# A transformer trunk on one core: a scheduler's table of durations is corrected, and the steps of the attention block stand in another order

## The chip, the core and the metric

The kernel runs on one core of one Trainium2 chip. The metric is the device time of one execution in microseconds (us). The core's engines are TensorE (PE in the profile; its weight loads are PEld), VectorE (DVE), ScalarE (ACT), GpSimd (POOL) and SyncE (SP, which issues the transfers). Each of them works through its own instructions in the order in which the kernel lists them, and waits where an instruction needs what another engine has not yet made.

## The reference, cut to what matters

Two layers over 256 tokens of width 1024. Both begin and end with a half-step SwiGLU (width 2816). Between these, layer 0 has a gated linear recurrence, layer 1 a differential attention whose keys and values come from the stream behind layer 0. The change moves the steps of this attention:

```python
q = (h @ w_q).reshape(B, S, N_HEADS, 2, HEAD_DIM)
q = apply_rope(rmsnorm(q, q_norm), cos, sin) * (HEAD_DIM ** -0.5)
...
        scores = jnp.einsum('bhcqd,bhckd->bhcqk', qb, k, preferred_element_type=jnp.float32)
        p = jax.nn.softmax(jnp.where(mask, scores, -jnp.inf), axis=-1)
        attn = p[:, :, 0] - lam * p[:, :, 1]
        return jnp.einsum('bhqk,bhkd->bhqd', attn, vf)
...
    o = rmsnorm(o, sub_norm, SUBLN_EPS) * (1.0 - lambda_init)
    return o.reshape(B, S, D_MODEL).astype(h.dtype) @ w_o
```

There are 8 heads of 2 maps each (c = 0 and 1 above), so every head has two softmaxes.

## The kernel before

Every weight is read once, in pieces of 128x2048 floats (`raw`), by transfers that SyncE issues. Each half piece (a granule) is split into a high and a low part: ScalarE casts it (`whi`), VectorE subtracts (`wlo`). TensorE multiplies the high part with both parts of the activations and the low part with the high one. Six granules fit at a time.

The program is written twice. In a first pass a `Recorder` takes down every instruction of four engines and SyncE with what it depends on, and a planner (`plan`) runs through them: it keeps a clock for each engine, computes from `cost` how long an instruction holds its engine (`pitch`) and when its result is there (`lat`, with 94 ns to reach another engine), and among what could start within 60 ns takes the instruction with the longest work behind it. Instructions of one engine count as following each other at their pitch, except where the pair is in `op.raw`: then the second waits for the first one's result. In the second pass the instructions are issued in the order so found. So the durations in `cost` set the order on every engine, and nothing else: they compute nothing.

What `cost` cannot set is which tiles come to life in which order, and so which share a buffer. This is the program's order, and in the attention block it is `ATT_STEPS`, a list written by hand:

- `Q0`, `Q1`, `K0`, `K1`, `V0`, `V1`: a projection for heads 0 to 3 or 4 to 7, both halves of the tokens, 48 matmuls of 512 columns into two banks. Behind a Q or K projection ScalarE and VectorE norm and rotate the result (`qk_post`), and TensorE transposes it, four transposes for each half of the tokens. GpSimd's power gives the factor of the norm (`fac`, `facq`).
- `S0` to `S5`: scores and softmax. S0 and S3 are the first 128 tokens for heads 0 to 3 and 4 to 7; S1, S2, S4 and S5 the last 128 tokens for two heads each (0 and 1, 2 and 3, 4 and 5, 6 and 7). Scores go into two banks, one for each map. VectorE writes the mask and takes the maxima (`mx`), ScalarE has one exponential for each head and map, with the factor and the maximum as operands of one number per token and with a sum taken along; VectorE joins the two maps, TensorE transposes the result, and ScalarE copies it out.
- `A0` to `A6`: probabilities times values for two heads (`av`), 6 matmuls; then four squares with a sum on ScalarE, a power on GpSimd (`ofr`), four scaled copies on ScalarE, four transposes on TensorE.
- `O0` to `O7`: what 128 rows of the output projection give, 8 times 3 matmuls of 256 columns. O0 and O1 need A0, O2 and O3 need A2, and so on. The last two come behind the list.

The buffers in which TensorE's results stand are eight banks: six named `mm`, two named `aux`. All instructions carry one line of the kernel, that of the helper which issues them (L379; the changed kernel is one line shorter there, so L378), so that the tiles tell them apart.

Of the kernel before, what the change touches and what calls it, by code (L numbers as in the profile page):

```python
# [32 lines left out]
    "G3m M0 E3 D1 H4a M1 M2 E4 M3 H6m O0 M4 E5 M5 W W O1 E6 M6 E7 O2 O3 M7"  # L33
).split()
ATT_STEPS = (
    "Q0mm K1mm K0mm S1mm Q1mm S0mm V0mm A0 S2mm A2 S3mm V1mm S4mm S5mm O0 A4 O1 A6 O2 O3 O4 O5"
).split()
REC_OUT = "0m 1m 23m 45m 67s"
ATT_OUT = "0m 1m 23m 45m 67s"
# [55 lines left out]
def is_ap(v):  # L95
    return hasattr(v, "tensor") and hasattr(v, "ap")


def width(v):
    n = 1  # L100
    for _, c in v.ap[1:]:
        n *= c
    return n
# [12 lines left out]
def sources(a, k):  # L116
    vals = list(a if "out" in k else a[1:]) + [v for n, v in k.items() if n not in ("out", "accum_out")]
    return [v for v in vals if is_ap(v)]


def cost(op):
    k, out = op.k, op.outs[0] if op.outs else None
    ins = sources(op.a, k)
    psum = [v for v in ins if v.space == bass.MemoryType.PSUM]
    n = width(out) if out is not None else 1
    if op.eng == "tensor":
        if op.fn == "transpose":
            return 109, 220
        m = width(k["rhs"])
        if k["rhs"].dtype == BF16:  # L130
            return m / 2.4 + 3, m / 2.4 + 175
        if k["rhs"].dtype == F32R:
            return 0.4508 * m + 2.6, 0.4508 * m + 165
        p = 4 * m / 2.4 + 3 if m > 8 else 222
        if k["lhsT"].ap[0][1] <= HD:
            p /= 2
        return p, p + 170
    if op.eng == "scalar":
        if op.fn == "preload_act_table":
            return 1294, 1283  # L140
        scaled = is_ap(k.get("scale")) or is_ap(k.get("bias"))
        p = n / 1.2 + ((65 + 20 * scaled) if psum else (100 + 85 * scaled))
        lat = n / 1.2 + (172 if psum else 195 + 90 * scaled)
        return (p + 93, lat + 200) if len(op.outs) > 1 else (p, lat)
    if op.eng == "vector":
        if op.fn in ("reduce_sum", "reduce_max"):
            n = width(ins[0])
        if op.fn == "tensor_copy":
            return n / 1.92 + 67, n / 1.92 + 155
        if op.fn == "memset":  # L150
            return n / 0.96 + 10, n / 0.96 + 50
        if op.fn == "tensor_tensor_scan":
            return n * 2 / 0.96 + 55, n * 2 / 0.96 + 140
        rate = 0.96
        if op.fn == "tensor_scalar" and not psum:
            rate = 1.92
        scalar = op.fn in ("tensor_scalar", "scalar_tensor_tensor") and len(ins) > (1 if op.fn == "tensor_scalar" else 2)
        return n / rate + (125 if scalar else 68), n / rate + (210 if scalar else 153)
    if op.eng == "gpsimd":
        if op.fn == "memset":  # L160
            return 30, 100
        if k.get("op") == ALU.pow:
            return 300 + 170 * n, 340 + 170 * n
        return 120 + 2.14 * n, 160 + 2.14 * n
    return 420, 0


class Recorder:
# [16 lines left out]
    def add(self, eng, fn, a, k):  # L185
        op = Op()
# [11 lines left out]
        for v, w in [(v, False) for v in ins] + [(v, True) for v in op.outs]:  # L198
# [9 lines left out]
            for j, l, h, ww in self.hist[name]:  # L208
                if (w or ww) and l < hi and lo < h:
                    self.depend(op, j)  # L210
                    if ww and not w:
                        op.raw.add(j)
            if w:
                self.hist[name] = [x for x in self.hist[name] if not (lo <= x[1] and x[2] <= hi)]
            self.hist[name].append((op.i, lo, hi, w))
# [944 lines left out]
```

## Time and profile before

| | |
|---|---|
| three timed runs | 941.09, 941.13, 947.8 us; median 941.13 |
| the execution in the profile | 941.77 us, of which its span (first to last instruction) is 939.9 |
| TensorE busy | 930.3 us, 99% of the span |
| VectorE, ScalarE, GpSimd busy | 77%, 62%, 3% |
| granted TensorE clock, mean | 0.998 |
| attention block on TensorE | from 636.71 us (first projection) to 751.77 us (first matmul of the last SwiGLU) |

Two matmuls that follow each other overlap, and their ends are modelled, so the busy share of TensorE says little of how fast it works; but where a row says that it was idle and for whom it waited, nothing ran on it. The distance from one matmul's start to the next one's is what a matmul costs.

### The profile page before, as it was taken

Reading aid. Unit: us, or ns where it says so; the run is one execution under the profiler, and the core shown is the slowest. Engines: PE = TensorE matmul, PEld = TensorE weight load, DVE = VectorE, ACT = ScalarE, POOL = GpSimd, SP = SyncE. Lnnn points to the kernel's source line nnn. Section 1 sums busy time; section 2 is a strip of 40 time slices with the busy share of each in tenths; the row PEclk is TensorE's granted clock in tenths of the full one; section 3 lists DMA queues with packets and bytes.
Section 4 is the critical chain, followed back from the end, with each engine's and each line's share of the span. In section 5 each row is a group of like instructions: output and inputs, shape, how many; then the busy total and the mean of one; then the engine's idle time right before and its main releaser. Section 6 shows DMA issues by size and latency. Waiting matters only on the chain.

```text
span 939.9 us, 14667 instructions
## 1 busy us (share of the span) xinstructions
PE 930.3 (99%) x5586; PEld 824.5 (88%) x5586; DVE 723.9 (77%) x1226; ACT 581.2 (62%) x1039; POOL 31.9 (3%) x42
## 2 busy tenths in 40 slices
PE   8999999999999999999999999999999999999998
PEld 7888888899998888888888888888877988888887
DVE  7898887679898888866688887667996598888651
ACT  7666565569975656555566556555579766565541
POOL 0200000000000000000000000001310000000000
PEclk9999999999999999999999999999999999999999
DMA  8755556534375555555555555555533445555540
GB/s 318 246 201 196 180 183 237 208 136 141 132 266 180 182 193 205 182 179 192 203 186 182 182 191 201 189 179 179 179 135 97 164 175 194 180 184 201 204 158 17
DMA packets 25991, 172.33 MB, mean 183 GB/s; under 512 B 3136, under 2 KB 4288, under 8 KB 5568
## 3 DMA queue, kind: packets, MB, share of 16 engines
q1 hardware_dynamic: 25920, 171.39, 52.0%
q8 instruction: 44, 0.72, 0.3%
q14 instruction: 27, 0.22, 0.1%
HBM read 170.33 MB, written 1.05 MB: 182 GB/s over the span
## 4 chain that ended last, share of the span: by engine, by line
PE 95%; ACT 3%; DVE 1%; DMA 0%; issue 0%; SPq 0%; ACTq 0%
PE mm L379 92%; PE aux L379 3%; ACT w L379 2%; ACT b L379 1%; DMA xa<-xT 0%; ACT whi L379 0%; DVE wlo L379 0%; ACT L379 0%; DVE mx L379 0%; DVE w L379 0%; ACT xs L379 0%; DVE xs L379 0%; DVE xa L379 0%; SPq L379 0%; DVE mm L379 0%
## 5 line engine op out<-in xcount | busy, mean ns | idle before, releaser
L379 PE MATMUL mm<-xs,whi 128*128 128x512 f32 (+1 forms) x1632 | 531.6, 378 | 2.0 <-DVE xs L379 2.0
L379 DVE TENSOR_TENSOR wlo<-raw,whi 128x1024 fp32r<-128x1024 f32 (+1 forms) x321 | 391.0, 1220 | 132.8 <-ACT whi L379 132.2
L379 ACT CAST whi<-raw 128x1024 fp32r<-128x1024 f32 (+1 forms) x321 | 335.5, 1047 | 200.5 <-PE mm L379 180.5
L379 PE MATMUL mm<-xs,wlo 128*128 128x256 f32 x1520 | 426.2, 281 | 0.0
L379 PEld LDWEIGHTS mm<-xs,whi 128*128 128x128 f32 x1632 | 298.9, 188 | 60.3 <-DVE xs L379 2.3
L379 PE MATMUL mm<-b,whi 128*128 128x512 f32 (+1 forms) x982 | 292.7, 359 | 0.3 <-ACT w L379 0.2
L379 PEld LDWEIGHTS mm<-xs,wlo 128*128 128x128 f32 x1520 | 287.9, 190 | 0.5
L379 PE MATMUL mm<-b,wlo 128*128 128x256 f32 x832 | 233.2, 281 | 0.0
L379 PEld LDWEIGHTS mm<-b,whi 128*128 128x128 f32 x982 | 174.7, 189 | 29.1 <-ACT w L379 0.9
L379 PEld LDWEIGHTS mm<-b,wlo 128*128 128x128 f32 x832 | 157.6, 189 | 0.0
L379 ACT ACTIVATE w<-mm 128x256 f32<-128x256 f32 x207 | 79.5, 385 | 115.4 <-PE mm L379 110.8
L379 DVE TENSOR_TENSOR w<-mm,w 128x256 f32<-128x256 f32 x176 | 73.5, 421 | 27.1 <-ACT w L379 27.0
L379 DVE TENSOR_TENSOR w<-w,rb 128x512 f32<-128x512 f32 x88 | 60.2, 687 | 0.4
L379 DVE TENSOR_TENSOR w<-w,w 128x256 f32<-128x256 f32 (+2 forms) x104 | 45.2, 440 | 0.6 <-ACT w L379 0.6
L379 PE MATMUL mm<-whi,xk 128*128 128x512 f32 x128 | 42.1, 400 | 0.0
L379 ACT ACTIVATE w<-w 128x256 f32<-128x256 f32 x88 | 36.5, 418 | 3.3 <-DVE w L379 2.9
L379 DVE TENSOR_TENSOR b<-w,b 128x256 fp32r<-128x256 f32 x88 | 36.4, 417 | 1.9 <-ACT b L379 1.9
L379 ACT CAST b<-w 128x256 fp32r<-128x256 f32 x88 | 35.4, 406 | 2.9 <-DVE w L379 2.8
L379 DVE SCALAR_TENSOR_TENSOR xa<-mm,xa 128x256 f32<-128x256 f32 x32 | 13.5, 423 | 26.8 <-PE mm L379 18.4
L379 PEld LDWEIGHTS mm<-whi,xk 128*128 128x128 f32 x128 | 24.0, 188 | 4.7
L379 PE MATMUL mm<-wlo,xk 128*128 128x512 f32 x64 | 25.2, 394 | 0.0
L379 ACT ACTIVATE xs<-xa,vt 128x256 fp32r<-128x256 f32 x40 | 19.7, 504 | 8.9 <-DVE xa L379 8.7
(124 smaller groups left out, 483.8 us busy)
## 6 DMA issues: line engine op xcount, KB each, us to landing
raw<-wts SPq DMA_DIRECT2D x159, 1024.0 KB, 4.8
raw<-wts SPq DMA_DIRECT2D x3, 512.0 KB, 7.3
outT<-xa SPq DMA_DIRECT2D x8, 128.0 KB, 2.0
xa<-xT SPq DMA_DIRECT2D x3, 256.0 KB, 6.5
raw<-wts SPq DMA_DIRECT2D x2, 256.0 KB, 4.4
rw<-rows SPq DMA_DIRECT2D x1, 320.0 KB, 4.9
xa<-xT SPq DMA_DIRECT2D x1, 260.0 KB, 4.3
ident<-eye SPq DMA_DIRECT2D x1, 64.0 KB, 8.6
```

The lines of the kernel that those rows point to most:

```text
L379: getattr(getattr(self.nc, op.eng), op.fn)(*op.a, **op.k)
```

## The change

In `cost` the numbers of four kinds of instruction are replaced: matmuls on split weights, ScalarE operations with operands of one number per token (each such operand now counts 83 ns in the pitch, where before the first or only one counted 20 ns on a source in a bank and 85 ns on one in SBUF, and a second one nothing), VectorE's memset, and with it the results' times. In `Recorder.add` every pair of accesses to the same tile of which one writes is now in `op.raw`, where before a pair was there only if the first wrote and the second read. And `ATT_STEPS` has the same 22 steps in another order.

```diff
 ATT_STEPS = (
-    "Q0mm K1mm K0mm S1mm Q1mm S0mm V0mm A0 S2mm A2 S3mm V1mm S4mm S5mm O0 A4 O1 A6 O2 O3 O4 O5"
+    "K0mm K1mm Q0mm Q1mm S1mm S0mm V0mm S4mm A0 S2mm S3mm A2 V1mm A4 S5mm O0 O1 O2 A6 O3 O4 O5"
 ).split()
...
         if k["rhs"].dtype == F32R:
-            return 0.4508 * m + 2.6, 0.4508 * m + 165
+            return 0.4428 * m + 3.3, 0.4428 * m + 165
...
-        scaled = is_ap(k.get("scale")) or is_ap(k.get("bias"))
-        p = n / 1.2 + ((65 + 20 * scaled) if psum else (100 + 85 * scaled))
-        lat = n / 1.2 + (172 if psum else 195 + 90 * scaled)
+        scalars = is_ap(k.get("scale")) + is_ap(k.get("bias"))
+        p = n / 1.2 + (65 if psum else 100) + 83 * scalars
+        lat = n / 1.2 + (172 if psum else 195) + 93 * scalars
         return (p + 93, lat + 200) if len(op.outs) > 1 else (p, lat)
...
         if op.fn == "memset":
-            return n / 0.96 + 10, n / 0.96 + 50
+            return max(15, n / 0.96 - 60), n / 0.96 + 40
...
                 if (w or ww) and l < hi and lo < h:
                     self.depend(op, j)
-                    if ww and not w:
-                        op.raw.add(j)
+                    op.raw.add(j)
```

What this does to the order is seen best at three places of the attention block. The numbers in the names only tell tiles apart, and differ between the two kernels.

The first place is ScalarE behind the projection V0. In the kernel before, `mm_1525` and `mm_1526` are the scores of S2, `mm_1541` and `mm_1542` those of S3, and `aux_1519` is the result of A0, whose scaled copies (`ofr`) are what TensorE transposes next:

```order
L379 ACTIVATE w_3_1529,sm_1528<-mm_1525,mx_1527,facq_0_1387 128x256
L379 ACTIVATE w_4_1522,oss_1520<-aux_1519,ra_1504 128x128
L379 ACTIVATE w_4_1522,oss_1520<-aux_1519,ra_1472 128x128
L379 ACTIVATE w_4_1522,oss_1520<-aux_1519,ra_1504 128x128
L379 ACTIVATE w_4_1522,oss_1520<-aux_1519,ra_1472 128x128
L379 ACTIVATE w_3_1529,sm_1528<-mm_1525,mx_1527,facq_0_1387 128x256
L379 ACTIVATE w_0_1530,sm_1528<-mm_1526,mx_1527,facq_0_1387 128x256 x2
L379 ACTIVATE w_5_1545,sm_1544<-mm_1541,mx_1543,facq_0_1388 128x128 x4
L379 ACTIVATE w_2_1546,sm_1544<-mm_1542,mx_1543,facq_0_1388 128x128 x4
L379 ACTIVATE w_4_1522<-aux_1519,ofr_1523 128x128 x4
```

In the changed kernel `mm_1519` and `mm_1520` are the scores of S4, `mm_1535` and `mm_1536` those of S2, `mm_1544` and `mm_1545` those of S3, and `aux_1529` is the result of A0:

```order
L378 ACTIVATE w_5_1523,sm_1522<-mm_1519,mx_1521,facq_0_1388 128x256 x2
L378 ACTIVATE w_1_1532,oss_1530<-aux_1529,ra_1504 128x128
L378 ACTIVATE w_1_1532,oss_1530<-aux_1529,ra_1494 128x128
L378 ACTIVATE w_1_1532,oss_1530<-aux_1529,ra_1504 128x128
L378 ACTIVATE w_1_1532,oss_1530<-aux_1529,ra_1494 128x128
L378 ACTIVATE w_2_1524,sm_1522<-mm_1520,mx_1521,facq_0_1388 128x256 x2
L378 ACTIVATE w_3_1539,sm_1538<-mm_1535,mx_1537,facq_0_1387 128x256 x2
L378 ACTIVATE w_0_1540,sm_1538<-mm_1536,mx_1537,facq_0_1387 128x256 x2
L378 ACTIVATE w_1_1532<-aux_1529,ofr_1533 128x128 x3
L378 COPY b_0_1528<-aux_1527 128x512
L378 ACTIVATE w_1_1532<-aux_1529,ofr_1533 128x128
L378 ACTIVATE w_4_1548,sm_1547<-mm_1544,mx_1546,facq_0_1388 128x128 x4
```

The four copies of A0 stood behind the eight exponentials of S3 and stand ahead of them now; S4's four exponentials, which came after V1 before, have been put in ahead of S2's.

The second place is TensorE in V0 (`mm_1507`, `mm_1508`), where the transposes of S0's probabilities (`aux_1506`) come in. Before:

```order
L379 MATMUL mm_1508<-wlo_1511,xk_644 128x512
L379 MATMUL mm_1508<-whi_1510,xk_644 128x512
L379 MATMUL aux_1506<-ident_79,w_2_1502 128x128
L379 MATMUL mm_1507<-wlo_1513,xk_644 128x512
L379 MATMUL aux_1506<-ident_79,w_2_1502 128x128
L379 MATMUL mm_1507<-whi_1512,xk_644 128x512
L379 MATMUL aux_1506<-ident_79,w_2_1502 128x128 x2
```

Now:

```order
L378 MATMUL mm_1508<-wlo_1511,xk_644 128x512
L378 MATMUL aux_1506<-ident_79,w_4_1502 128x128
L378 MATMUL mm_1508<-whi_1510,xk_644 128x512
L378 MATMUL aux_1506<-ident_79,w_4_1502 128x128 x2
L378 MATMUL mm_1507<-whi_1512,xk_644 128x512
L378 MATMUL aux_1506<-ident_79,w_4_1502 128x128
L378 MATMUL mm_1507<-wlo_1513,xk_644 128x512
```

They come behind V0's 41st matmul, and came behind its 37th. The transposes of S1's probabilities and of Q1's second half, which before came behind the 20th and the 27th, come behind the 32nd and 33rd now.

The third place is TensorE right behind the scores of S0 (`mm_1498`, `mm_1499`). Before, V0 follows at once, and the first transposes of Q1's result come 19 matmuls later:

```order
L379 MATMUL mm_1499<-b_0_1383,b_0_1381 128x128
L379 MATMUL mm_1498<-b_0_1383,b_0_1381 128x128
L379 MATMUL mm_1499<-b_0_1383,b_0_1381 128x128
L379 MATMUL mm_1507<-whi_1484,xk_644 128x512
L379 MATMUL mm_1507<-wlo_1485,xk_644 128x512
```

Now the first transposes of Q1's result (`aux_1482`) stand between:

```order
L378 MATMUL mm_1499<-b_0_1383,b_0_1381 128x128
L378 MATMUL mm_1498<-b_0_1383,b_0_1381 128x128
L378 MATMUL mm_1499<-b_0_1383,b_0_1381 128x128
L378 MATMUL aux_1482<-ident_79,w_1_1480 128x128 x4
L378 MATMUL mm_1507<-whi_1474,xk_644 128x512
```

So a step of VectorE that has Q1's result to rotate is waited for 19 matmuls earlier. Outside the attention block TensorE's order differs in some 30 rows of the recurrent block and in a few of the SwiGLU blocks; ScalarE's and VectorE's differ by neighbours that change places, and SyncE's transfers come in the same order throughout.

## Rows read from the trace of the kernel before

**Rows 1.** The page: TensorE's busy time; shares of the chain that ended last.

```profile
PE 930.3 (99%) x5586; PEld 824.5 (88%) x5586; DVE 723.9 (77%) x1226; ACT 581.2 (62%) x1039; POOL 31.9 (3%) x42
...
PE 95%; ACT 3%; DVE 1%; DMA 0%; issue 0%; SPq 0%; ACTq 0%
```

**Rows 2.** Busy time by stretch: length, each engine (instructions), granted clock, DMA.

```profile
0.00:12.00 12.00, 8.98 (x39) 6.99 (x40) 6.33 (x15) 8.40 (x16) 0.34 (x6) 0.86 0.82 284
12.00:660.00 648.00, 647.92 (x3905) 578.31 (x3904) 513.78 (x844) 406.21 (x687) 16.12 (x25) 1.00 0.55 193
660.00:700.00 40.00, 39.06 (x200) 31.25 (x199) 37.75 (x79) 26.67 (x52) 10.74 (x6) 1.00 0.42 148
700.00:720.00 20.00, 18.25 (x111) 14.69 (x111) 14.34 (x40) 16.98 (x55) 2.01 (x2) 1.00 0.45 156
720.00:740.00 20.00, 19.71 (x161) 18.27 (x158) 12.20 (x32) 17.72 (x52) 1.01 (x1) 1.00 0.32 109
740.00:939.90 199.90, 196.40 (x1182) 175.02 (x1180) 139.49 (x219) 105.20 (x184) 1.70 (x2) 1.00 0.47 164
```

**Rows 3.** Timeline of TensorE around V0's end: start, length, operation [idle before <- releaser].

```profile
697.47 0.30 PE L379 MATMUL aux<-ident,w 128*128 128x128 f32 x1 [0.78 <-DVE w L379]
...
700.26 0.40 PE L379 MATMUL mm<-whi,xk 128*128 128x512 f32 x1
700.59 2.02 PE L379 MATMUL mm<-b,b 64*128 64x256 f32 x24
702.54 1.60 PE L379 MATMUL aux<-b,b 128*128 128x128 f32 x12
703.90 0.48 PE L379 MATMUL mm<-whi,xk 128*128 128x512 f32 x1
...
711.15 0.85 PE L379 MATMUL aux<-ident,w 128*128 128x128 f32 x3 [1.75 <-ACT w L379]
```

**Rows 4.** Timeline of ScalarE in V1: S2's first exponential to A0's copies.

```profile
703.58 0.56 ACT L379 ACTIVATE w<-mm,mx,facq 128x256 f32<-128x256 f32 x1 [1.26 <-DVE mx L379]
...
704.18 0.37 ACT L379 ACTIVATE w<-aux,ra 128x128 f32<-128x128 f32 x1
...
706.65 0.58 ACT L379 ACTIVATE w<-mm,mx,facq 128x256 f32<-128x256 f32 x1
...
707.20 0.48 ACT L379 ACTIVATE w<-mm,mx,facq 128x128 f32<-128x128 f32 x1
...
710.67 1.20 ACT L379 ACTIVATE w<-aux,ofr 128x128 f32<-128x128 f32 x4
711.67 1.14 ACT L379 CAST whi<-raw 128x1024 fp32r<-128x1024 f32 x1
...
713.18 0.70 ACT L379 COPY b<-aux 128x512 f32<-128x512 f32 x1
```

**Rows 5.** Timeline of TensorE: SwiGLU (56 pairs of matmuls between the first two), a projection.

```profile
25.25 0.39 PE L379 MATMUL mm<-xs,whi 128*128 128x512 f32 x1
...
44.66 0.39 PE L379 MATMUL mm<-xs,whi 128*128 128x512 f32 x1
...
637.18 0.62 PE L379 MATMUL mm<-whi,xs 128*128 128x512 f32 x2
...
646.73 0.62 PE L379 MATMUL mm<-whi,xs 128*128 128x512 f32 x2
```

**Rows 6.** Timeline of TensorE in V0: transposes between matmuls.

```profile
690.72 0.60 PE L379 MATMUL aux<-ident,w 128*128 128x128 f32 x4
691.07 0.48 PE L379 MATMUL mm<-whi,xk 128*128 128x512 f32 x1
691.39 0.83 PE L379 MATMUL aux<-ident,w 128*128 128x128 f32 x4
```

**Rows 7.** Timeline of VectorE: two products on Q1's first half, the second one in place.

```profile
684.33 0.69 DVE L379 TENSOR_TENSOR w<-w,gs 128x512 f32<-128x512 f32 x1
685.05 0.69 DVE L379 TENSOR_TENSOR w<-w,gc 128x512 f32<-128x512 f32 x1
```

## The prediction

> **What bounds the kernel now.** I read the page first: TensorE is busy 99% of the span, and 95% of the chain that ended last is its own work [rows 1]. So a gain can only come from time in which TensorE stands still, or from fewer changes between kinds of matmul on it. The busy times by stretch say where it stands still [rows 2]. From 12 to 660 us it is idle for 0.08 us in 648. At the start it is idle for 3.02 us and at the end for 3.50 (the first transfers and the last stores, whose instructions the change leaves in their order). In between lie three stretches of the attention block: 0.94 us in 660 to 700, 1.75 in 700 to 720 and 0.29 in 720 to 740, together **2.98 us**. That is all that the change can win back in idle time, 0.3% of the kernel.
>
> The timeline of TensorE names the two large pieces [rows 3]. At 697.47 S0's transposes waited 0.78 us for VectorE, which joins the two maps once ScalarE's exponentials are done. At 711.15 A0's transposes waited 1.75 us for ScalarE. The timeline of ScalarE says why [rows 4]: A0's four copies began at 710.67, directly behind S3's eight exponentials, which had held ScalarE since 707.20, and nobody waited for those eight.
>
> **Whether the new durations are the traced ones.** S3's eight exponentials took 710.67 - 707.20 = 3.47 us, 0.434 each [rows 4]. The old formula gives 128/1.2 + 65 + 20 + 93 = 285 ns, the new one 128/1.2 + 65 + 2 x 83 + 93 = 431. An exponential of 256 columns took 0.55 [rows 4], by the formulas 391 and 537 ns. Four scaled copies took 1.00 us; old 4 x 192 = 0.77, new 4 x 255 = 1.02. So the old planner believed that S3's exponentials took 8 x 0.149 = 1.2 us less than they do, and put A0's copies behind them. That is the hole at 711.15. A pair of SwiGLU matmuls took 19.41 us / 56 = 346.6 ns [rows 5]; old 351.4, new 346.7. An overwrite in place on the same engine began 0.72 us after the instruction that still read the data, which is 0.69 long [rows 7]: it waits for the result, as the new rule has it. The numbers are better ones, and they meet the mistake that made the large hole.
>
> **What goes.** Where V1 runs, ScalarE now has S4's and S2's exponentials, then A0's copies, then S3's. I check that A0's copies come in time by summing from V0's end. In the trace V0's last matmul starts at 700.26 and takes 0.23, so its end is 700.49, and the first exponential of the next softmax starts at 703.58, 3.1 us later [rows 3, 4]; S4 has the same chain of mask and maximum before it. Then come 8 exponentials of 0.55 and 4 squares of 0.37 [rows 4], 5.9 us, so that the copies begin 9.0 us behind V0's end; four of them take 1.0, and the copy of S4's probabilities between them about 0.5, so the last is done at 10.5. TensorE reaches A0's transposes after the scores of S4, S2 and S3 (8 matmuls of 256 columns and 8 of 128; 4 and 8 of these take 2.02 us [rows 3], so about 3.0), A0's six (703.90 - 702.54 = 1.36), 26 of V1's matmuls at 9.55 us / 42 = 0.227 [rows 5], which is 5.9, and S4's four transposes (691.07 - 690.72 = 0.35 [rows 6]): 10.6 us. That is 0.1 us behind the last copy: this hole closes, with nothing to spare. S0's transposes stand behind four more matmuls of V0 (0.9 us against a wait of 0.78), and what stood ahead of them on ScalarE and VectorE is the same: this hole closes as well. The rest of the 2.98 us are pieces of 0.1 to 0.2; I let them go too. **Term A: -2.98 us.**
>
> **What comes.** (1) TensorE changes from matmuls to transposes more often: in the attention block 29 times by the order, 25 before. Such a change costs the matmul ahead 691.39 - 691.07 - 0.227 = 0.09 us [rows 6]. **Term B: 4 x 0.09 = +0.36.** (2) Q1's first transposes now stand directly behind the scores of S0. The last matmul of Q1's first half ends 3 x 0.227 = 0.68 us ahead of Q1's end. Behind it follow ScalarE's copy (0.70 [rows 4]), two products (0.72 each) and a sum (0.69) on VectorE [rows 7]; the order puts two short masks ahead of the sum, and with these and the ways between engines I add 0.6, an estimate. 0.70 + 1.44 + 0.69 + 0.6 - 0.68 = 2.75 us behind Q1's end, against 2.02 us of scores: TensorE waits 0.7. The least is nothing (the masks start late, so the sum may pass early); the most is about 1.7, if VectorE is still held by the factor that it gets from GpSimd. **Term C: +0.7.** (3) Elsewhere each group of transposes has cover by the same kind of sum, but little of it (0.1 to 0.4 us at A0's and S4's groups in V1, at A2's, A4's and S5's in the output projection). **Term D: +0.2**, between 0 and 1.5.
>
> **What costs nothing.** In the SwiGLU blocks the order changes between neighbours on ScalarE and VectorE; TensorE was idle for 0.08 us in 648 there [rows 2], because a granule is split while earlier ones are still used, and a neighbour's 0.4 us does not reach that cover. In the recurrent block two groups of small matmuls stand some 24 matmuls later; what ScalarE makes of them came 6 us later anyhow, and the block had no hole to win. K0 ahead of Q0 changes which of two ready inputs is read first, and GpSimd's powers follow: K's four come first, then that of the stream's norm, then Q's; between Q0's end and the first use of its factor, in S1's maxima, lie Q1's 48 matmuls (10.9 us). SyncE's transfers keep their order, and none is waited for in the block.
>
> **Sum.** -2.98 + 0.36 + 0.7 + 0.2 = -1.7 us. Against the profiled execution's own 941.77 us (span 939.9 and 1.87 around it) that is 940.1; that execution lies 0.64 above the median of the runs, 941.13, so I forecast **939.4**.
>
> **The rivals.** *The holes only move* (0.22): the cover in V1 and in the output projection was 0.1 to 0.4 us in my sums; if five of these places miss by 0.3 each and C is 1.2, then C and D are 2.7 us in place of 0.9, and the time is 941.2. For it speaks that ScalarE is busy 85% of the stretch in which the holes lie [rows 2]; against it that the planner now counts the same durations as the trace.
>
> *Slower, since ScalarE comes late through V1* (0.1): S4's four exponentials (2.2 us) are new ahead of S3's. By the sum above S3's exponentials end 10.5 + 3.5 = 14.0 us behind V0's end, and the joined map is there some 0.8 later, at 14.8; TensorE comes to its transposes after 44 of V1's matmuls, 3.0 + 1.36 + 10.0 + about 1.3 for twelve transposes = 15.7. The cover is 0.9 us. Since the transposes stand between A2's matmuls, TensorE can do nothing else there. From 0.9 + 1.7 = 2.6 us of lateness on the kernel is slower than before; at 4 us, as from three casts of 0.95 that get ahead or from a late factor for heads 4 to 7 (S4 is the first to need it, 10 us earlier than before), it is 939.4 + 3.1 = 942.5.
>
> *A lost clock* (0.03): from 0 to 12 us the mean granted clock is 0.86 [rows 2], which is a part of the stretch at the lower of the two levels, 1.2 GHz, behind an idle piece of TensorE; in the attention block it stays at 1.00 through the hole of 1.75 us. If the new order has an idle piece that brings the clock down once, then 0.14 x 2 x 12 = 3.4 us run at half speed, which costs 1.7 us: 941.1. The Trainium skill's page "TensorE: Matmul & The Clock Gate", Part 1 (The HAM clock gate), has it that the clock is halved after an idle spell and comes back with sustained work; by that rule a hole of 1.75 us could have cost as much again, and closing it would give back 1.7 us more, but the trace shows no such loss there.
>
> *It does not do what it says* (0.05): the same waits appear under other names, and the time stays at 941.1. Against it stands that A0's copies have changed sides with S3's exponentials.
>
> **How the numbers follow.** The forecast has 0.6, its own range is 938.1 (A alone, with a little more from the recurrent block) to 940.5. For 8 in 10 I take in the case of moved holes and most of the slower one: 937.6 to 942.5. One per cent is 9.4 us, about what a measurement of this kernel can tell from no change. All the idle time inside the kernel is less than a third of that, so faster by over 1% has 0.01. For slower by over 1% TensorE would have to stand still for four times what it does now in that block; I leave 0.03. Within 1%: 0.96.
>
> **What would show it.** In the changed kernel's profile: idle time of TensorE from 660 to 740 us of about 1 us instead of 2.98; no wait for ScalarE of over 0.5 us at A0's transposes; a wait of 0.3 to 1 us at the transposes behind S0's scores; the first matmul of the last SwiGLU near 750 us instead of 751.77; the other stretches as they are. I am wrong if a wait of over 1 us stands in V1 or in the output projection, if the granted clock falls below 1.00 between 20 and 930 us, or if TensorE is idle in the SwiGLU blocks.

## The result, and the profile after

The changed kernel takes 936.76 us in the median of its executions (935.07 to 939.56), the kernel before 941.50 in the same comparison (940.74 to 947.8). The ratio is 0.9947, with a 95% interval of 0.9932 to 0.9962. That is 4.7 us less where 1.7 were forecast, and 0.84 us below the lower end of the wider range (937.6). The traced execution of the changed kernel took 939.56 us (span 937.5); eight of the fourteen lie between 935.1 and 936.9. In the traced one the first SwiGLU makes that difference, as shown below; the other thirteen have no trace. One execution of the run before_copies (below) took 1747.9 us at a granted clock of 0.86, and no ratio here counts it.

First the page, which answers to [rows 1], then the busy time by stretch, which answers to [rows 2] (length, each engine with its instructions, granted clock, DMA):

```profile
PE 930.3 (99%) x5586; PEld 823.8 (88%) x5586; DVE 723.0 (77%) x1226; ACT 579.0 (62%) x1039; POOL 31.1 (3%) x42
...
PE 94%; DVE 3%; POOL 1%; DMA 1%; issue 0%; ACT 0%; SPq 0%; ACTq 0%
```

```profile
0.00:12.00 12.00, 8.81 (x41) 6.17 (x42) 6.17 (x15) 8.26 (x16) 0.34 (x6) 1.00 0.80 281
12.00:660.00 648.00, 647.91 (x3886) 576.24 (x3885) 513.08 (x843) 402.57 (x682) 13.27 (x24) 1.00 0.55 192
660.00:700.00 40.00, 39.47 (x212) 32.52 (x211) 37.40 (x80) 28.18 (x56) 12.79 (x7) 1.00 0.41 142
700.00:720.00 20.00, 20.00 (x128) 16.82 (x127) 15.03 (x47) 17.61 (x55) 1.01 (x1) 1.00 0.37 138
720.00:740.00 20.00, 20.00 (x167) 19.40 (x166) 13.07 (x28) 18.20 (x53) 2.53 (x3) 1.00 0.50 166
740.00:937.50 197.50, 194.06 (x1162) 172.67 (x1161) 138.28 (x217) 104.14 (x181) 1.19 (x2) 1.00 0.47 165
```

TensorE is idle for 0.53 us from 660 to 740 instead of 2.98. But the busy time is the same 930.3 us in both, and from 12 to 660 us TensorE runs 19 matmuls fewer in the same 648 us. Both are odd if idle time is all that a change can win. Two things stand behind them: waits that the idle view does not show, which the prediction missed, and the pace of the first SwiGLU.

TensorE's timeline behind S0's scores and at A0's transposes, and ScalarE's at A0's copies, answer to [rows 3, 4]:

```profile
686.28 2.03 PE L378 MATMUL mm<-b,b 64*128 64x256 f32 x24
688.81 0.63 PE L378 MATMUL aux<-ident,w 128*128 128x128 f32 x4 [0.51 <-DVE w L378]
...
698.38 0.27 PE L378 MATMUL aux<-ident,w 128*128 128x128 f32 x1
698.40 0.48 PE L378 MATMUL mm<-whi,xk 128*128 128x512 f32 x1
698.72 0.38 PE L378 MATMUL aux<-ident,w 128*128 128x128 f32 x2
...
712.29 0.39 PE L378 MATMUL mm<-whi,xk 128*128 128x512 f32 x1
712.53 1.03 PE L378 MATMUL aux<-ident,w 128*128 128x128 f32 x8
713.32 0.47 PE L378 MATMUL mm<-whi,xk 128*128 128x512 f32 x1
```

```profile
710.98 0.92 ACT L378 ACTIVATE w<-aux,ofr 128x128 f32<-128x128 f32 x3
711.73 0.65 ACT L378 COPY b<-aux 128x512 f32<-128x512 f32 x1
712.19 0.46 ACT L378 ACTIVATE w<-aux,ofr 128x128 f32<-128x128 f32 x1
712.45 0.54 ACT L378 ACTIVATE w<-mm,mx,facq 128x128 f32<-128x128 f32 x1
```

The wait of Term C is there: the last matmul of S0's scores starts at 688.03, the transposes at 688.81, a distance of 0.78. A0's transposes follow at 712.53, directly behind the last copy, with no wait.

**Waits that the idle view hides.** A matmul of 512 columns is shown busy for 0.39 us, but in an unbroken row the next one starts 0.227 us after it [rows 3, 5]. So a wait of up to some 0.16 us is not shown as idle time, and a longer one is shown that much too short. One of them in the kernel before:

```profile
725.64 0.40 PE L379 MATMUL mm<-b,whi 128*128 128x256 f32 x2
725.88 0.28 PE L379 MATMUL mm<-b,wlo 128*128 128x256 f32 x1
726.27 0.50 PE L379 MATMUL mm<-b,whi 128*128 128x256 f32 x2
```

The distance from 725.88 to 726.27 is 0.39 us, where 0.117 is usual, and not even a mark of idle time stands there. I listed all distances from start to start between the first projection and the statistics of the last SwiGLU. These fourteen are waits, with what each has over the usual distance, in ns:

```
651 us 145   669 us 245   681 us 242   692 us 122   696 us 947   709 us 1906   711 us 149
711 us 149   724 us 320   725 us 163   726 us 277   730 us 174   736 us 123    744 us 122
```

Together 5.08 us; the idle view has 2.98 there, which is 0.15 less for each, on average. The changed kernel has two left, 725 ns at 688 and 183 at 696 us. The recurrent block, with 0.08 us of idle time, had two such waits (at 225 and 257 us, 0.58 us with the matmuls behind them); the changed kernel has none. The Trainium skill's page "Perfetto Trace Analysis", section "Tensor Engine Instruction (MATMUL, LD_WEIGHTS)", says that the profiler computes TensorE's end times and does not measure them; the 0.39 against 0.227 us agrees.

**The pace of a SwiGLU block.** [Rows 5] have 346.6 ns for a pair of matmuls in the first SwiGLU. In the traced execution of the changed kernel 59 pairs take 20.85 us, 353.4 ns each; when the same kernel was traced again (run after_again) they take 20.46, 346.8 each. The timeline of TensorE, first the one, then the other:

```profile
24.96 0.40 PE L378 MATMUL mm<-xs,whi 128*128 128x512 f32 x1
...
45.81 0.40 PE L378 MATMUL mm<-xs,whi 128*128 128x512 f32 x1
```

```profile
25.23 0.40 PE L378 MATMUL mm<-xs,whi 128*128 128x512 f32 x1
...
45.69 0.39 PE L378 MATMUL mm<-xs,whi 128*128 128x512 f32 x1
```

The granted clock is 1.00 in both, and the idle view shows no wait. At 353.4 ns the whole block takes 179.85 us instead of 176.5.

**By stages.** Taken from start to start on TensorE, between the broadcasts of the statistics and the first projection of the attention block (whose stage here holds the first 14.5 us of the last SwiGLU as well), the traces divide as follows. "Idle" is the idle view's time in the attention stage; the last columns are medians, and ratios to the kernel before, which ran beside each (its medians: 941.8 beside the runs from order_only to pitch_only, 942.3 on a second chip, 944.7 to 944.8 on three others). A ratio compares all executions and is not the quotient of the two medians. The other columns are of one trace each.

| kernel | first SwiGLU | recurrent | attention | idle there | last SwiGLU | median | ratio (95%) |
|---|---|---|---|---|---|---|---|
| before | 176.42 | 83.35 | 129.52 | 2.97 | 169.89 | 941.50 | |
| after | 179.85 | 82.50 | 124.48 | 0.53 | 169.89 | 936.76 | 0.9947 (0.9932 to 0.9962) |
| order_only | 179.72 | 83.79 | 141.66 | 11.19 | 169.89 | 957.05 | 1.0172 (1.0140 to 1.0205) |
| costs_only | 176.53 | 82.50 | 141.19 | 10.47 | 172.99 | 955.72 | 1.0150 (1.0136 to 1.0164) |
| no_pitch | 176.48 | 82.78 | 127.42 | 2.64 | 169.88 | 938.84 | 0.9969 (0.9959 to 0.9979) |
| pitch_only | 176.53 | 83.36 | 130.43 | 2.57 | 169.89 | 942.46 | 1.0001 (0.9991 to 1.0012) |
| no_act | 176.53 | 82.75 | 139.35 | 10.11 | 169.89 | 951.18 | 1.0087 (1.0068 to 1.0105) |
| no_raw | 176.53 | 82.97 | 124.92 | 0.58 | 173.00 | 940.05 | 0.9971 (0.9961 to 0.9981) |
| before_copies2 | 179.73 | 83.35 | 129.54 | 2.77 | 173.00 | 944.76 | 1.0000 (0.9986 to 1.0015) |
| before_fill | 176.48 | 83.35 | 129.03 | 2.44 | 169.89 | 943.55 | 0.9987 (0.9966 to 1.0008) |
| after_q1 | 176.53 | 82.50 | 124.53 | 0.27 | 173.00 | 939.13 | 0.9962 (0.9948 to 0.9976) |
| after_again | 176.53 | 82.50 | 124.56 | 0.55 | 173.00 | 938.98 | 0.9925 (0.9910 to 0.9941) |
| after_third | 176.53 | 82.50 | 124.56 | 0.53 | 173.00 | 938.82 | 0.9928 (0.9910 to 0.9945) |
| after_bc | 176.30 | 82.50 | 124.55 | 0.55 | 173.00 | 939.00 | 0.9926 (0.9910 to 0.9942) |
| after_bc4 | 176.53 | 82.50 | 124.65 | 0.52 | 169.77 | 936.33 | 0.9924 (0.9903 to 0.9946) |
| after_bc04 | 176.30 | 82.50 | 124.69 | 0.50 | 169.77 | 935.72 | 0.9913 (0.9894 to 0.9933) |
| after_bc04_b | 176.30 | 82.50 | 124.67 | 0.55 | 169.77 | 936.12 | 0.9897 (0.9881 to 0.9914) |
| after_q1_bc | 176.53 | 82.50 | 124.66 | 0.30 | 169.77 | 935.86 | 0.9893 (0.9876 to 0.9911) |
| before_bc4 | 176.49 | 83.36 | 129.69 | 3.05 | 169.77 | 943.02 | 0.9991 (0.9974 to 1.0008) |

The second and third SwiGLU, 353.7 us together, are alike in all. So the change is worth -5.04 in attention and -0.85 in the recurrent stage (0.24 of it are two matmuls that now stand on the other side of its border), 5.65 us in all. The 3.4 us more in the first SwiGLU are not shown to belong to the change: order_only and before_copies2, in which the broadcast there stands where the kernel before has it, took them too.

### The profile page after: what moved, and what is told of

The parts are those of the page before. It is cut to its first block, busy times and chain, and to the rows that moved or that the text cites. A ratio compares the mean times of both kernels' runs of the same rounds, so it can differ in the third digit from the quotient of the medians.

```text
span 937.5 us, 14663 instructions
## 1 busy us (share of the span) xinstructions
PE 930.3 (99%) x5586; PEld 823.8 (88%) x5586; DVE 723.0 (77%) x1226; ACT 579.0 (62%) x1039; POOL 31.1 (3%) x42
## 4 chain that ended last, share of the span: by engine, by line
PE 94%; DVE 3%; POOL 1%; DMA 1%; issue 0%; ACT 0%; SPq 0%; ACTq 0%
PE mm L378 92%; PE aux L378 2%; DVE w L378 1%; DVE wlo L378 1%; DMA xa<-xT 1%; DVE ss L378 0%; POOL facq L378 0%; POOL fac L378 0%; POOL rt_mix L378 0%; ACT w L378 0%; SPq L378 0%; ACT whi L378 0%; ACT xs L378 0%; DVE fac L378 0%; DVE xa L378 0%
```

## The experiments

### Parts of the change

Each of these takes a part of the diff, with nothing else.

**order_only**: the list of steps alone, with the old durations.

```diff
-    "Q0mm K1mm K0mm S1mm Q1mm S0mm V0mm A0 S2mm A2 S3mm V1mm S4mm S5mm O0 A4 O1 A6 O2 O3 O4 O5"
+    "K0mm K1mm Q0mm Q1mm S1mm S0mm V0mm S4mm A0 S2mm S3mm A2 V1mm A4 S5mm O0 O1 O2 A6 O3 O4 O5"
```

> Only the new list of attention steps, all durations as before. Main theory: TensorE's waits in the attention block go because of the list (before, distances from start to start exceed the usual ones by about 5 us of waits there; the idle view shows 2.98). From the first query matmul to the statistics of the last SwiGLU it then takes 123 us instead of 126.7, the first SwiGLU keeps its 346.7 ns per pair of matmuls, the recurrent block its 83.0 us; time 937.5. Rival: it is the durations that close the holes, since with the old ones the planner still puts long exponentials ahead of A0's or A2's copies; then the block stays at 125.5 or more and the time at 940 to 941.

Measured: 957.05, and 141.66 us of attention. Both theories were far off: the list alone is 15 us slower than the kernel before. In the traces 12.1 us of that are attention and 3.3 the pace of the first SwiGLU. Three waits of 2.8 to 3.7 us and one of 1.1 stand in V1 and in the output projection, all for ScalarE. With two of them the granted clock fell (busy time by stretch, as above):

```profile
740.00:760.00 20.00, 12.67 (x84) 11.37 (x83) 10.63 (x21) 13.06 (x29) 1.01 (x1) 0.84 0.26 90
760.00:780.00 20.00, 20.00 (x121) 18.39 (x121) 16.13 (x34) 13.24 (x26) 0.48 (x1) 0.91 0.43 167
```

That is (0.16 + 0.09) x 2 x 20 = 10.0 us at 1.2 GHz, 5.0 us lost at most: up to that much of the 12.1 us is a slower TensorE and not a wait. The traces of costs_only and no_act have as much of it (granted clock 0.96 over the attention stage in all three).

**costs_only**: the durations alone, with the old list.

```diff
+            return 0.4428 * m + 3.3, 0.4428 * m + 165
+        scalars = is_ap(k.get("scale")) + is_ap(k.get("bias"))
+        p = n / 1.2 + (65 if psum else 100) + 83 * scalars
+            return max(15, n / 0.96 - 60), n / 0.96 + 40
+                    op.raw.add(j)
```

> Only the new durations (ScalarE, matmul pitch, memset, overwrites), the old list of attention steps. Main theory: the durations alone move A0's copies ahead of eight exponentials and close the wait of 1.9 us, and shorten the recurrent block by 0.6; but they also put the broadcast of the first SwiGLU's statistics one matmul later, ahead of a 512-column matmul, and in a part of the executions its pairs then take 353.3 instead of 346.7 ns, 3.4 us in all: 938.5 where they don't, 942 where they do. Rival (the list does it all): attention as before, so 941 and more in every execution.

Measured: 955.72, 14 us slower; in the traces 11.7 us are attention, with the lost clock, and 3.1 the pace of the last SwiGLU. The main theory fell with it: A0's transposes, which waited 1.75 us in the kernel before, now wait 5.6 us for ScalarE's copies (three more waits for ScalarE have 1.3 us each):

```profile
724.38 0.48 PE L378 MATMUL aux<-ident,w 128*128 128x128 f32 x1 [5.60 <-ACT w L378]
```

So neither the list nor the truer durations alone close the holes. Only together do they give a good order: the list fits the planner that has these durations. One thing came as expected: the recurrent block has its 82.50 us with the durations alone.

**no_pitch**, **pitch_only**: all but the matmul pitch, and the pitch alone.

```diff
-            return 0.4508 * m + 2.6, 0.4508 * m + 165
+            return 0.4428 * m + 3.3, 0.4428 * m + 165
```

> The changed kernel with the old matmul pitch (0.4508 m + 2.6), all else changed. Main theory: the pitch alone moves the broadcast in the first SwiGLU; here it stands ahead of a 256-column matmul as in the kernel before, so all executions have 346.7 ns per pair there, none has the 3.4 us more; attention gains 5 us, the recurrent block 0 instead of 0.6; time 936.2 with all executions within 1 us. Rival: the slower pairs of the first SwiGLU come from the start (there TensorE ran at full clock from its first matmul, in the kernel before 3.4 us at half), so executions spread over 3.5 us here too.

> The kernel before with the new matmul pitch alone. Main theory: the broadcast in the first SwiGLU moves ahead of a 512-column matmul, and a part of the executions takes 353.3 ns per pair there (3.4 us more); the recurrent block gives 0.6 back, attention stays within 1 us of before: 940.5 where pairs take 346.7, 944 where they take 353.3. Rival (the start or the list causes the slower pairs): every execution within 1 us of 941.

Measured: attention 127.42 and 130.43, so the pitch is worth 2.9 us of the block together with the rest. Alone it took 0.9 more, but its trace has a stretch at half the clock that can cost as much (below), so no cost of the pitch alone is shown. The theory on the first SwiGLU fell: the pitch does move the broadcast there, but pitch_only had 176.5 us in its trace, order_only, which leaves the broadcast where it was, 179.7, and one of no_pitch's eight executions, without a trace, took 942.2 against 938.2 to 939.1 for the others.

**no_act**, **no_raw**: the changed kernel with the old ScalarE durations, and with the old rule for overwrites.

```diff
-        scalars = is_ap(k.get("scale")) + is_ap(k.get("bias"))
+        scaled = is_ap(k.get("scale")) or is_ap(k.get("bias"))
```

```diff
-                    op.raw.add(j)
+                    if ww and not w:
+                        op.raw.add(j)
```

> The changed kernel with the old ScalarE durations (list, pitch, memset and overwrites new). With the list alone the attention block took 141.7 us, with all but the pitch 127.4, with everything 124.5. Theory (the durations of the exponentials are what the list needs): without them the planner again puts exponentials ahead of A's copies, and the block takes over 132 us, the recurrent block about 83.3; time over 944. Rival (pitch and overwrites do most of it): the block stays under 128 us, time 940 or less.

> The changed kernel with the old rule for overwrites on one engine (list, ScalarE durations, pitch and memset new). Theory: the rule matters for little in attention, since TensorE waits for ScalarE there and the rule speaks of read data overwritten in place; the block stays within 1 us of 124.5, and the recurrent block, whose order on ScalarE and VectorE the rule changes, loses its gain (82.5 to 83.3 us); time up to 1 us above the changed kernel. Rival (the list fits one plan only, and any other number breaks it): the block takes 127 us or more, time over 939.

Measured: 139.35 us of attention without ScalarE's durations (951.18), 124.92 without the rule (940.05): in attention as the theories had it. The recurrent block lost less than they said (82.75 and 82.97 us; 83.3 was expected). The list rests on ScalarE's durations above all. The rule is worth 0.4 in attention and 0.5 in the recurrent block. That no_raw lies 3.3 us above the changed kernel, where 1 was expected, is its last SwiGLU, which took 3.1 more.

### Single orders, with everything else held

The next kernels change the list of operations that the planner gives out, on one engine, just ahead of its emission. The diffs are of that engine's order.

**before_copies**, **before_copies2** (the same kernel, the second time for its trace): ScalarE, A0's copies ahead of four exponentials.

```diff
 ACTIVATE w_5,sm<-mm,mx,facq_0 128x128 x4
+ACTIVATE w_4<-aux,ofr 128x128 x4
 ACTIVATE w_2,sm<-mm,mx,facq_0 128x128 x4
-ACTIVATE w_4<-aux,ofr 128x128 x4
```

> The kernel before with one change in the order that its planner gives out: on ScalarE A0's four scaled copies stand ahead of the last four of S3's eight exponentials instead of behind them; every other engine's order is as before. Theory (the large hole is ScalarE's order alone): the factor is ready on VectorE at 708.7 and the copies could start at 708.9 instead of 710.67, so the distance of 2133 ns at A0's transposes falls to about 400, the attention block from 129.5 to 127.8 us and the time by 1.7 to about 939.8. Rival (holes only move): S3's last exponentials end 1.0 us later, what follows on ScalarE too, and the waits come back in the output projection; the block stays above 129 us and the time at 941 or more.

> The kernel of the run before_copies once more, for a trace at full clock. Its executions took 941.5, as the kernel before (941.4) in its quicker ones. Either the wait at A0's transposes is gone and 1.7 us are lost elsewhere: as a slower pace of the last SwiGLU (173.0 instead of 169.9 us, as in the runs costs_only, after_q1 and no_raw; then the attention block takes 127.8 or less), or as waits that moved (the block is back at 129.5, with new distances over 300 ns in the output projection). Or the wait did not go: the distance at A0's transposes is still over 1.5 us.

Measured: 941.51 (0.9988 of the kernel before beside it, 0.9978 to 0.9999) and 944.76 (1.0000); attention 129.54. The wait at A0's transposes is gone (412 ns from 711.86 to 712.27), and a new one stands at the products behind them. TensorE, then ScalarE (without its accumulator reads):

```profile
711.86 0.39 PE L418 MATMUL mm<-wlo,xk 128*128 128x512 f32 x1
712.27 0.85 PE L418 MATMUL aux<-ident,w 128*128 128x128 f32 x3
...
714.89 0.40 PE L418 MATMUL mm<-whi,xk 128*128 128x512 f32 x1
716.80 0.38 PE L418 MATMUL aux<-b,b 128*128 128x128 f32 x1 [1.51 <-ACT b L418]
```

```profile
711.79 1.20 ACT L418 ACTIVATE w<-aux,ofr 128x128 f32<-128x128 f32 x4
712.79 0.55 ACT L418 ACTIVATE w<-mm,mx,facq 128x128 f32<-128x128 f32 x1
...
714.54 1.15 ACT L418 CAST whi<-raw 128x1024 fp32r<-128x1024 f32 x1
715.47 0.80 ACT L418 ACTIVATE b<-aux,vt 128x512 fp32r<-128x512 f32 x1
716.05 0.70 ACT L418 COPY b<-aux 128x512 f32<-128x512 f32 x1
```

The products need the copy at 716.05, and ahead of it in ScalarE's queue stands the same work as before, in another order. The rival "holes only move" holds for this edit.

**before_fill**: TensorE, work at hand ahead of the wait. The eight transposes and the products that stood among V1's matmuls come behind 14 of these.

```diff
+MATMUL mm<-whi,xk 128x512
 ...
 MATMUL aux<-ident,w_4 128x128 x4
 MATMUL aux<-ident,w_3 128x128 x4
-MATMUL mm<-whi,xk 128x512
 ...
 MATMUL aux<-b_0,b_0 128x128
```

> The kernel before with TensorE's order alone changed: A0's transposes, S3's transposes and the six products that stood among V1's matmuls from 711 to 715 us now stand behind 14 of those matmuls (3.2 us of work at hand). Theory (the wait is lack of ordered work, and that is what the new list supplies by placing V1 behind A2): distances over 300 ns vanish there, the attention block falls from 129.5 to about 127.7 us, the time by 1.8 below the kernel before on the same chip. Rival (ScalarE is the bound through this stretch and the wait comes back): the block stays at 129 or more, with new distances over 300 ns at S4's or S5's steps in the output projection.

Measured: attention 129.03, 0.5 less. The 1.9 us became waits of 0.98 and 0.70 further on (0.32 stood at the second place before), both for ScalarE:

```profile
714.82 0.38 PE L429 MATMUL aux<-b,b 128*128 128x128 f32 x1 [0.82 <-ACT b L429]
...
724.14 0.39 PE L429 MATMUL mm<-b,whi 128*128 128x256 f32 x1 [0.54 <-ACT w L429]
```

**after_q1**: TensorE, the changed kernel's wait of Term C filled.

```diff
+MATMUL mm<-whi,xk 128x512
+MATMUL mm<-wlo,xk 128x512
+MATMUL mm<-whi,xk 128x512
+MATMUL mm<-whi,xk 128x512
 MATMUL aux<-ident,w_1 128x128 x4
```

> The changed kernel with four transposes moved on TensorE: Q1's first ones, directly behind S0's scores, now stand behind four of V0's matmuls (0.9 us of work); every other engine's order is the same. Theory (the wait of 0.73 us there is a plain wait for VectorE's sum): it is filled, the attention block goes from 124.5 to 123.8 us, the time 0.7 below the changed kernel. Rival (the copy behind the transposes comes 0.15 us later, and ScalarE's exponentials behind it are what the next transposes wait for): the wait comes back within the next 10 us, and the block stays at 124.4 or more.

Measured: attention 124.53, no less than 124.48 to 124.56. The 0.73 us are gone and 0.40 come back at the next transposes, where the idle view has 0.24 (the rest of the 0.73 is not placed):

```profile
691.26 0.41 PE L418 MATMUL aux<-ident,w 128*128 128x128 f32 x2 [0.24 <-DVE rm L418]
```

The time of 939.13 is explained by the last SwiGLU, which took 173.0 us.

### The pace of the first and the last SwiGLU

**after_again**, **after_third**: the changed kernel as it is (no edit), on two chips.

> The changed kernel as it is, once more. Theory: executions of about 935.5, 936.6 and 939.2 us, which differ by the pace of the first SwiGLU alone (346.7, 348.2 or 353.3 ns per pair: 176.5, 177.3 or 179.8 us); the attention block takes 124.5, the recurrent 82.5, the last SwiGLU 169.9 in each. Rival: the executions differ in the attention block, by waits that come and go.

> The changed kernel as it is, beside the run after_bc04_b on the same chip. Theory (the pace of the first and the last SwiGLU is drawn at their broadcasts): executions near 935.7, 936.6 or 939.1 us, by the pace of one or both blocks; attention 124.5 us. Rival (chips differ, places don't): the same time as after_bc04_b.

Measured: 938.98 and 938.82, attention 124.56 in both. The theory for after_again, that the first SwiGLU alone makes the difference, fell: here the first is at 346.8 ns and the last at 353.4, 61 pairs in 21.56 us in after_again.

```profile
790.18 0.40 PE L378 MATMUL mm<-xs,whi 128*128 128x512 f32 x1
...
811.74 0.40 PE L378 MATMUL mm<-xs,whi 128*128 128x512 f32 x1
```

**after_bc**, **after_bc4**, **after_bc04**, **after_bc04_b** (the one before, again), **before_bc4**, **after_q1_bc**: the broadcast one matmul later on TensorE, in the first SwiGLU (bc), the last (bc4, after_q1_bc) or both (bc04). The first:

```diff
+MATMUL mm<-xs_0,whi 128x512
 MATMUL aux<-w_7,ones 128x256
-MATMUL mm<-xs_0,whi 128x512
 MATMUL mm<-xs_0,wlo 128x256
```

The last:

```diff
+MATMUL mm<-xs_0,wlo 128x256
 MATMUL aux<-w_0,ones 128x256
-MATMUL mm<-xs_0,wlo 128x256
 MATMUL mm<-xs_0,whi 128x512
```

> The changed kernel with the broadcast of the first SwiGLU's statistics one matmul later on TensorE, behind the 512-column matmul and ahead of the 256-column one, as it stands in the kernel before and in the other SwiGLU blocks. Theory (the pace of a SwiGLU block is drawn at this broadcast and kept to its end; ahead of the 256-column matmul it comes out at 346.7 ns per pair in most executions): the first block takes 176.5 us in most executions, the time is 935.5, with few at 939. Rival (the place has nothing to do with it): executions lie between 935 and 939.5 as those of the changed kernel do.

> The changed kernel with the broadcast of the last SwiGLU one matmul later, ahead of a 512-column matmul. Theory (the pace is drawn at the broadcast, from how it meets the matmuls around it, and this place draws 346.7 or 348.2 ns per pair): the last SwiGLU takes 169.9 to 170.6 us, time 935.5 to 936.5 where the first SwiGLU is quick, whatever the changed kernel does on this chip. Rival (chance): 173.0 us there on a chip on which the changed kernel has 169.9, or no pattern.

> Both broadcasts moved, that of the first SwiGLU ahead of a 256-column matmul (as in the run after_bc, where the block took 176.3 us), that of the last ahead of a 512-column one (as in after_q1_bc, 169.8 us). Theory: both blocks quick in most executions, 935.5 us with little spread, the best of all kernels here. Rival: one of them at 353.3 ns per pair, 939.

> The changed kernel with both broadcasts moved, once more, beside the changed kernel. Theory: 935.2 to 936.6 us in every execution, first SwiGLU 176.3, last 169.8, and so 0 to 3.3 us below the changed kernel on the same chip, by the pace that this one draws there. Rival: executions at 938 and over here too.

> The kernel before with the broadcast of the last SwiGLU one matmul later. Theory (the pace has nothing to do with the change): the last SwiGLU takes 169.9 to 170.6 us and the time is 941.4 to 942 where the first block is quick, so the change's own part, attention and the recurrent block, is 5.8 us when both kernels run at the same pace. Rival: 173.0 us there, 944.7, in this kernel.

> The kernel of the run after_q1 with the broadcast in the last SwiGLU one matmul later, ahead of a 512-column matmul. In after_q1 the last SwiGLU ran at 353.3 ns per pair in its trace (173.0 us), and all executions lay within 1.3 us. Theory (the pace is drawn at the broadcast from how it meets the matmuls around it): another place draws anew, and the block takes 169.9 or 170.6 us; time 935 to 936. Rival (the pace was fixed earlier, by the attention block's end): 173.0 again, 939.

Measured: with the last broadcast moved, the last SwiGLU took 169.77 us in all five traces, of both kernels, on three chips. Unmoved it took 169.9 in seven of the other traces above and 173.0 in seven. All executions agree on the two chips where both were run: 11 with the last broadcast moved took 935.1 to 936.8 us (after_q1_bc, after_bc04_b), 18 of the changed kernel with it unmoved (after_bc among them) 938.4 to 940.4. So after_bc missed its forecast of 935.5 by the last block. The places do not settle every execution: one of after_bc4 took 939.6, and six of before_bc4's twelve 943.1 to 946.1 where 941.4 to 942 were expected; which stage was slow in these no trace shows.

The traces also say where the pace changes. All nineteen, of either kernel, enter the last SwiGLU at 353.3 ns a pair, and up to this broadcast (at 763.89 us in the changed kernel's trace) they keep it. Directly behind the broadcast twelve run at 346.7 and seven stay at 353.3. The trace of the changed kernel is one of the twelve, with 21 pairs in 7.42 us ahead of it and 60 in 20.80 behind it:

```profile
749.78 0.40 PE L378 MATMUL mm<-xs,whi 128*128 128x512 f32 x1
...
757.20 0.40 PE L378 MATMUL mm<-xs,whi 128*128 128x512 f32 x1
...
780.04 0.39 PE L378 MATMUL mm<-xs,whi 128*128 128x512 f32 x1
...
800.84 0.39 PE L378 MATMUL mm<-xs,whi 128*128 128x512 f32 x1
```

In after_bc04_b 64 pairs take 22.19 us, 346.7 ns each:

```profile
789.68 0.40 PE L428 MATMUL mm<-xs,whi 128*128 128x512 f32 x1
...
811.87 0.40 PE L428 MATMUL mm<-xs,whi 128*128 128x512 f32 x1
```

For the first SwiGLU the place decides nothing that these runs show: after_bc has 176.30 us, but nearly all other traces have the same pace there (176.4 to 176.5). after_bc04_b ran beside after_third on one chip: 936.12 against 938.82 us, 2.7 less with the same work, and no execution of the one reaches the other's. So on that chip the kernel with both broadcasts moved is quicker than the changed one, and than the kernel before.

## Why the prediction was wrong

**The step that failed** is the sentence "That is all that the change can win back in idle time", and with it the size of Term A. The direction was right: the two large holes close, and what was worked out for these two places held. But the 2.98 us were read from a view whose end times are modelled. By the distances the waits were 5.08 us in attention and 0.58 in the recurrent block. With 5.66 in place of 2.98 the same sum gives -4.4 us: 937.4 for the traced execution and 936.7 for the median; measured were 936.76. That this meets so well is in part luck: the stages give -5.65 at equal pace, 1.25 more than -4.4, and the median is one over executions of different paces.

**Term by term.** A: -2.98 forecast; -5.66 by the distances. B: +0.36 forecast; near nothing by the rows. The 0.09 us that the matmul behind a transpose takes longer are there, but the last transpose of each group gives them back: the matmul starts 0.02 to 0.03 us after it, where one transpose starts 0.11 after the other (eight of them take 713.32 - 712.53 = 0.79). A lone transpose and the matmul behind it take 698.72 - 698.38 = 0.34 us together, 0.11 + 0.227, so four more changes cost next to nothing. The reading took one half of the change for the whole. C: +0.7 forecast, 0.73 measured. D: +0.2 forecast, 0.18 measured (at 696 us). Some 0.9 us more are gained in many small distances, which are not all taken apart; a good part stands right behind the waits (in the kernel before, the matmul behind each of the three waits at 724 to 726 us came 0.22 us later in place of 0.12).

**The sum for A0's copies** held: 10.5 us behind V0's end for the last copy and 10.6 for TensorE's arrival; V0's last matmul ends at 701.80, and the two came 10.65 and 10.7 later.

**"Nobody waited for those eight"** was wrong, as before_copies2 shows. The hole was no misplaced group of copies but ScalarE's whole queue through V1, and neither of the two edits of one engine's order (before_copies, before_fill) closed it. Nor do the durations alone meet "the mistake that made the large hole": with them and the old list that wait is 5.6 us (costs_only). What closes it in the changed kernel is the new order of all engines; which step of the list does most of that was not tried, since the list works only with its own durations.

**What costs nothing.** "The block had no hole to win" failed for the recurrent block by the same view: two hidden waits, 0.58 us. That a neighbour's place in a SwiGLU block costs nothing holds for waits, but the time of such a block can differ by 3 us without a wait.

**The rivals.** A lost clock did not happen in the trace of the changed kernel, whose granted clock is 1.00 in every stretch. It did happen with either list in order_only, costs_only and no_act, behind longer waits, and in pitch_only the wait at A0's transposes (1.73 us by the idle view) is followed by a stretch at half the clock:

```profile
700.00:720.00 20.00, 18.27 (x104) 15.35 (x104) 13.41 (x37) 15.84 (x53) 2.01 (x2) 0.91 0.46 158
```

0.09 x 2 x 20 = 3.6 us at 1.2 GHz cost 1.8 at most. The traced execution of the kernel before kept its clock at the same wait of 1.75 us. The Trainium skill's page "TensorE: Matmul & The Clock Gate", Part 1 (The HAM clock gate), has the clock halved after an idle spell. For this wait one trace agrees and the other does not. A lost clock may have struck the kernel before in many executions: beside order_only and no_act, 23 of its 44 had a mean granted clock of 0.998 and medians of 942.7 and 942.8 us, against 941.4 and 941.5 for the others. All fourteen executions of the changed kernel in the first comparison had 0.999 or 1.00. Where those 23 lost it is not shown; in the one traced execution of the kernel before with 0.998 it was at the start [rows 2]. "The holes only move" is right for the single-engine edits of the kernel before that were tried, and wrong for the change.

## What to carry to other kernels

Measure waits on TensorE from start to start against the usual distance of the same pair, and not by idle time: fourteen waits were shown 0.15 us too short on average, 2.1 us in all, of a miss of 3.0. A list of steps and the durations of the planner that reads it are one thing; either half of this change alone made the attention block 12 us longer, up to 5 of them by a lower clock. Before a difference of a few us is given to an edit, compare stages that the edit does not touch: here a block of unchanged work was 3.1 to 3.4 us longer or not.

## What the hardware showed that was not expected

An alternating row of 512- and 256-column matmuls, with no idle time shown and the granted clock at 1.00, runs at one of two paces, 346.7 or 353.3 ns a pair, and in the first and the last SwiGLU the block keeps the pace that it has behind the broadcast, 14 to 17 us from its start. The changed kernel differed from trace to trace, in the first SwiGLU (179.85 us in one, 176.53 in two others) and in the last (169.89 in the one, 173.00 in the two). In the last block the pace before the broadcast is 353.3 ns in every trace, so the broadcast is where a block gets quicker or does not, and its place goes with which it is. What decides at the unmoved place is open: it gave both paces.

A few transposes between matmuls cost little more than their own time: 0.34 us for a lone transpose and the matmul behind it, against 0.11 and 0.227 in unbroken rows.
